# One layout of PSUM banks for the whole program, and the second block's seven products each in a bank of its own

## The chip, the cores and the metric

The kernel runs on one core of a Trainium2 chip. The metric is the time of one execution in microseconds (us) on the device, as the median of several runs. The engines are named as the profile names them: PE (TensorE, matrix products; PEld is its loading of weights), DVE (VectorE), ACT (ScalarE), POOL (GpSimd) and SP (SyncE, which issues the DMAs). Products accumulate in PSUM, which has eight banks of 128 x 512 fp32 numbers here; PE writes them, DVE and ACT read them.

## The reference

Two transformer-like blocks of two layers each run one after the other on 512 tokens of width 1024, in fp32. The first block mixes differential attention with a linear recurrence and ends each layer with a gated feed-forward part. The change concerns only the second block:

```python
for l in range(DEPTH):                               # DEPTH = 2
    mix = hybrid_mixer(x, positions, ...)
    x = layer_norm(ALPHA * x + mix, ...)
    cross = memory_cross_attention(x, mem, ...)
    x = layer_norm(ALPHA * x + cross, ...)
    h = jnp.square(jax.nn.relu(x @ w_ff1[l]))         # 1024 -> 4096
    x = layer_norm(ALPHA * x + h @ w_ff2[l], ...)     # 4096 -> 1024
```

## The kernel before

Activations lie transposed, as eight tiles of 128 features by 512 tokens. An fp32 product is made of three matmuls on float32r operands: high times high, high times low, low times high (`mm3`, L105 to L108). So each weight tile of 128 x 1024 is loaded by a DMA on SP, its high part cast on ACT (`whi`) and its low part subtracted on DVE (`wlo`); the normalised activations have their high and low parts too (`xh_all`, `xl_all`).

The feed-forward part of a layer works in four parts of 1024 hidden features each. A part computes its hidden features (the up products), passes them through relu and square into the pairs `y0` to `y3`, and then runs eight down products of 24 matmuls of 512 columns, which add into the residual `hall` (L750). Most up products go by Strassen's scheme in Winograd's form: two weight tiles and the activations are cut into quarters, and seven products of quarters take the place of eight. `halves4` (L146) makes the sums of weights, on POOL (L155 to L158), and their high and low parts. `turn_operand` (L1180) makes the sums of activations once per layer: for k from 0 to 3, POOL forms `tt` (L1189 to L1192), ACT casts its high part `th` and DVE its low part `tl` (L201, L202). `tt` has one buffer, so the second k waits until the first is cast. `seven` (L172) runs the products: each is 12 matmuls of 256 columns, 84 in all. Parts 1 to 3 have four sevens each. Part 0 begins with four plain products (`up`, L1209), three of them in halves of 256 tokens, since the norm before it finishes its halves one after the other, and has two sevens: fourteen per layer, twenty-eight in all.

A framework schedules the instructions of each engine into one order ahead of time, gives tiles their buffers in rotation and adds the semaphores. Each engine runs its own list strictly in order. PSUM banks come from a pool by name: three banks `mm`, two `sc`, and one each of `tr`, `av` and `bc`. The feed-forward part of the second block has a pool of its own, `psum_f`: three pairs of banks `two`, one `av` and one `bc`. It is opened at L1226, and the usual layout is opened again after layer 0 (L1234). A new pool hands out nothing until the last reader of the old one's banks is done. Within `psum_f`, `bank("mm")` hands out a pair in two halves, one per product, and a pair is free when both halves have been read. Part 0 leaves an odd count of halves in use, so from there on one pair is held over from the last down product of a part to the first of the next, and two pairs are left for the sevens.

In `seven`, the first product goes to `av`, and ACT copies it into `u`. The other six fill three pairs, which DVE reads two banks at a time: L190 (products 1 and 2, named p26), L193 (p57, and L194 of 256 columns) and L197 (p34). With two pairs, p34 takes the pair that p26 of the same seven had.

Of the kernel before, what the change touches and what calls it, by code (L numbers as in the profile page):

```python
# [46 lines left out]
def both_blocks(ctx: ExitStack, tc: tile.TileContext, xT, cst, par1, w1in, w1out, w1gu, w1dn, wgate,  # L47
# [2 lines left out]
    consts = ctx.enter_context(tc.tile_pool(name="consts", bufs=1))  # L50
    wpool = ctx.enter_context(tc.tile_pool(name="w", bufs=1))
    res = ctx.enter_context(tc.tile_pool(name="res", bufs=1))
    banks = ExitStack()
    psum = None

    def open_psum(name):
        nonlocal psum, banks, paired, halves
        paired, halves = name == "psum_f", None
        banks.close()
        banks = ExitStack()  # L60
        psum = banks.enter_context(tc.tile_pool(name=name, bufs=1, space=bass.MemoryType.PSUM))

    open_psum("psum")
    EARLY = 4
    BANKS = {"mm": 3, "sc": 2, "tr": 1, "av": 1, "bc": 1}
    EXTRA = {"mix1": None, "ff1": None, "mix2": "tr", "cross": "tr", "ff2": None}
    extra, turns, paired = None, {}, False

    ALL = [(0, 264), (264, 528)]
    REAL = [(16, 528)]  # L70
# [36 lines left out]
        nc.tensor.matmul(ps, wh, xl, start=False, stop=False)  # L107
        nc.tensor.matmul(ps, wl, xh, start=False, stop=last)  # L108

    halves = None  # L110

    def bank(name):
        nonlocal halves
        if name == "mm" and paired:
            if halves is None:
                got = psum.tile([128, 2, 512], F32, name="two", bufs=3)
                halves = got[:, 1]
                return got[:, 0]
            got, halves = halves, None
            return got  # L120
        n = turns[name] = turns.get(name, 0) + 1
        if name == extra and n % (BANKS[name] + 1) == 0:
            name = "bc"
        return psum.tile([128, 512], F32, name=name, bufs=BANKS[name])
# [12 lines left out]
            got.append((ps[:, :b - a], a, b))  # L137
        return got

    def twice(p):  # L140
        return p[:, None, :].to_broadcast([128, 2, p.shape[1]])

    def pair_of_banks():
        return psum.tile([128, 2, 512], F32, name="two", bufs=3)

    def halves4(pool, w1, w2):  # L146


        r1 = wpool.tile([128, 8, 128], F32, name="wraw", bufs=3)
        nc.sync.dma_start(r1, w1)  # L150
        r2 = pool.tile([128, 8, 128], F32, name="wraw2", bufs=2)
        nc.sync.dma_start(r2, w2)
        s = pool.tile([128, 8, 128], F32, name="ws", bufs=1)
        s4 = pool.tile([128, 4, 128], F32, name="ws4", bufs=1)
        nc.gpsimd.tensor_add(s[:, 4:], r2[:, :4], r2[:, 4:])  # L155
        nc.gpsimd.tensor_sub(s[:, :4], s[:, 4:], r1[:, :4])
        nc.gpsimd.tensor_sub(r2[:, :4], r1[:, :4], r2[:, :4])
        nc.gpsimd.tensor_sub(s4, r1[:, 4:], s[:, :4])  # L158
        got = []
        for x in (r1, s, r2, s4):  # L160
            if x is s4:
                hi = pool.tile([128, 4, 128], F32R, name="wh4", bufs=1)
                lo = pool.tile([128, 4, 128], F32R, name="wl4", bufs=1)
            else:
                hi = wpool.tile([128, 8, 128], F32R, name="whi", bufs=3)
                lo = wpool.tile([128, 8, 128], F32R, name="wlo", bufs=3)
            nc.scalar.copy(hi, x)  # L167
            (nc.gpsimd if x is s4 else nc.vector).tensor_sub(lo, x, f(hi))  # L168
            got += [(hi[:, o:o + 4], lo[:, o:o + 4]) for o in range(0, hi.shape[1], 4)]
        return got  # L170

    def seven(pool, w, x, n):  # L172


        a11, a12, s2, s1, s3, a22, s4 = w
# [3 lines left out]
            for k in range(4):  # L179
                mm3(ps, w[0][:, k], w[1][:, k], x[0][k], x[1][k], k == 0, k == 3)  # L180

        e = pool.tile([128, 4, n], F32, name="quarters", bufs=2)
        u = pool.tile([128, n], F32, name="u1", bufs=2)
        p1 = bank("av")[:, :n]
        p26, p57, p34 = (pair_of_banks()[:, :, :n] for _ in range(3))
        product(p1, a11, b11)
        nc.scalar.copy(u, p1)
        product(p26[:, 0], a12, b21)
        product(p26[:, 1], s2, t2)
        nc.vector.tensor_add(e[:, 0:4:3], p26, twice(u))  # L190
        product(p57[:, 0], s1, t1)
        product(p57[:, 1], s3, t3)
        nc.vector.tensor_add(e[:, 1:3], p57, twice(e[:, 3]))  # L193
        nc.vector.tensor_add(e[:, 3], p57[:, 0], e[:, 2])  # L194
        product(p34[:, 0], s4, b22)
        product(p34[:, 1], a22, t4)
        nc.vector.tensor_add(e[:, 1:3], p34, e[:, 1:3])  # L197
        return e

    def split(hi, lo, x):  # L200
# [493 lines left out]
    def two(t, k, a, b):  # L694
        return t[:, k:k + 2, a:b]

    def products(ms, spans, w, xs, evac):
        for sp in spans:
            for m in ms:
# [15 lines left out]
    with blk2:  # L715
# [135 lines left out]
        for l in range(2):  # L851
# [320 lines left out]

            with ExitStack() as ffn:
                share("ff2")
                open_psum("psum_f")
                ff = ffn.enter_context(tc.tile_pool(name="ff", bufs=1))
                before = ln
                ln = Norm(ff, LN_G + 16, LN_B + 16, l == 1)
# [21 lines left out]
                for part in range(4):  # L1200
# [20 lines left out]
                    for i in range(0 if part else 2, 4):  # L1221
                        with ExitStack() as order:
                            if part == 0:
                                for ins in after:
                                    order.enter_context(tc.issue_after(ins.ins))
                            w = halves4(ff, ups[part](2 * i), ups[part](2 * i + 1))  # L1226
                        e = seven(ff, w, rhs, 256)
                        squares(e.rearrange("p a b -> p (a b)"), *(t.rearrange("p a b -> p (a b)") for t in yp[i]))
                    phase(8, lambda m: w2f2[l, m, :, 8 * part:8 * part + 8], ys,
                          lambda m, p, a, b: ln.add(m, p, a, b, part == 0, part == 3),  # L1230
                          tail=3 if part == 3 else 0,
                          close=lambda *x: ln.close(*x, ahead=[] if l else [(wins[1], m) for m in HEAD]))
            if l == 0:
                open_psum("psum_m")  # L1234
            else:
                banks.close()


def _tiles(w):
# [106 lines left out]
```

## Time and profile before

| | |
|---|---|
| median of 3 runs | 2922.9 us (2922.8 to 2923.22) |
| profiled execution | 2924.1 us, span 2922.3 us, clock 0.981 |
| PE busy | 2775.8 us, 95% of the span |
| PEld busy | 2464.4 us, 84% |
| DVE busy | 1875.1 us, 64% |
| ACT busy | 1308.7 us, 45% |
| POOL busy | 520.8 us, 18% |
| chain that ended last | PE 79%, DVE 10%, issue 4%, ACT 4%, POOL 2% |

PE is busy nearly all the time, so what an edit is worth is read from the places where PE waits. In a row of the timeline, the bracket at the end gives how long the engine stood idle before the instruction, and which instruction ended the wait. Busy times of PE are from modelled ends, so the distance between the starts of matmuls says more than their durations.

### The profile page before, as it was taken

What the parts mean: (1) busy time and instruction counts of PE and PEld (TensorE: products, weight loads), DVE (VectorE), ACT (ScalarE), POOL (GpSimd) and SP (SyncE); (2) the same over time, 40 slices, a digit from 0 to 9 for tenths busy, and PEclk for the clock granted to TensorE, in tenths of its full rate; (3) what the DMA queues carried; (4) which work ended last, traced back from release to release, by engine and by line L of the source; (5) the groups of instructions that cost most, each with busy time, mean ns of one, the idle gap of its engine ahead of it and who ended that gap; (6) DMA issues with size and microseconds to landing.
All of it is one profiled execution on the core that took longest, in us unless ns stands there. A gap on an engine that the chain in (4) does not pass through costs nothing.

```text
span 2922.3 us, 45493 instructions
## 1 busy us (share of the span) xinstructions
PE 2775.8 (95%) x17556; PEld 2464.4 (84%) x17556; DVE 1875.1 (64%) x3662; ACT 1308.7 (45%) x2246; POOL 520.8 (18%) x521
## 2 busy tenths in 40 slices
PE   8989999999999999999999969999899999799998
PEld 7989999999877888887889868888777897688887
DVE  7887434457887444469976564556789775655555
ACT  6665222236665222236755343344456553434433
POOL 0111000000120000012120152233322200533442
PEclk9999999999999999999999989999899999899999
DMA  4232322333323333336233213332253241132322
GB/s 149 82 82 82 93 89 87 94 99 90 95 73 106 94 93 98 92 108 173 80 96 124 66 64 96 94 104 85 66 159 107 76 148 57 63 94 94 101 80 66
DMA packets 96505, 277.35 MB, mean 95 GB/s; under 512 B 13345, under 2 KB 20001, under 8 KB 96289
## 3 DMA queue, kind: packets, MB, share of 16 engines
q1 hardware_dynamic: 96288, 274.45, 31.1%
q8 instruction: 139, 2.28, 0.3%
q14 instruction: 78, 0.63, 0.1%
HBM read 241.82 MB, written 2.10 MB: 83 GB/s over the span
## 4 chain that ended last, share of the span: by engine, by line
PE 79%; DVE 10%; issue 4%; ACT 4%; POOL 2%; DMA 1%; SPq 0%; ACTq 0%; DVEq 0%; POOLq 0%
PE mm L107 17%; PE mm L108 17%; PE mm L106 17%; PE two L106 6%; PE two L107 6%; PE two L108 6%; PE av L106 1%; PE av L107 1%; PE av L108 1%; DVE wlo L102 1%; PE av L241 1%; ACT whi L167 1%; DVE isc L973 1%; DVE hall L804 1%; POOL quarters L1213 1%
## 5 line engine op out<-in xcount | busy, mean ns | idle before, releaser
L100 ACT CAST whi<-wraw 128x1024 fp32r<-128x1024 f32 (+2 forms) x404 | 406.7, 1007 | 836.1 <-PE mm L107 485.6
L106 PE MATMUL mm<-xh_all,whi 128*128 128x264 f32 (+2 forms) x2192 | 719.7, 329 | 13.5 <-ACT xh_all L340 6.7
L107 PE MATMUL mm<-xl_all,whi 128*128 128x264 f32 (+2 forms) x2192 | 720.1, 329 | 0.5 <-DVE xl_all L341 0.5
L108 PE MATMUL mm<-xh_all,wlo 128*128 128x264 f32 (+2 forms) x2192 | 717.9, 328 | 0.0
L102 DVE TENSOR_TENSOR wlo<-wraw,whi 128x1024 fp32r<-128x1024 f32 (+2 forms) x381 | 472.2, 1240 | 114.2 <-ACT whi L100 112.0
L106 PEld LDWEIGHTS mm<-xh_all,whi 128*128 128x128 f32 x2192 | 415.6, 190 | 46.0 <-ACT xh_all L340 6.7
L108 PEld LDWEIGHTS mm<-xh_all,wlo 128*128 128x128 f32 x2192 | 416.5, 190 | 30.0
L107 PEld LDWEIGHTS mm<-xl_all,whi 128*128 128x128 f32 x2192 | 415.4, 190 | 31.3 <-DVE xl_all L341 1.0
L107 PE MATMUL mm<-yl,whi 128*128 128x264 f32 (+1 forms) x528 | 169.3, 321 | 0.1
L108 PE MATMUL mm<-yh,wlo 128*128 128x264 f32 (+1 forms) x528 | 169.3, 321 | 0.0
L106 PE MATMUL mm<-yh,whi 128*128 128x264 f32 (+1 forms) x528 | 168.3, 320 | 0.0
L106 PE MATMUL two<-xh_all,whi 128*128 128x256 f32 (+1 forms) x336 | 101.3, 301 | 26.0 <-ACT quarters L1212 18.4
L673 DVE TENSOR_TENSOR su<-mm,rbc 128x264 f32<-128x264 f32 (+1 forms) x66 | 34.2, 519 | 139.8 <-PE mm L108 139.8
L682 DVE TENSOR_TENSOR hall<-hall,mm 128x264 f32<-128x264 f32 (+1 forms) x72 | 37.0, 514 | 119.9 <-PE mm L108 119.9
L750 DVE TENSOR_TENSOR hall<-hall,two 128x512 f32<-128x512 f32 (+1 forms) x54 | 33.8, 627 | 121.5 <-PE two L108 121.2
L107 PEld LDWEIGHTS mm<-yl,whi 128*128 128x128 f32 x528 | 99.2, 188 | 8.8 <-DVE yl L202 0.6
L108 PEld LDWEIGHTS mm<-yh,wlo 128*128 128x128 f32 x528 | 99.2, 188 | 7.3
L106 PEld LDWEIGHTS mm<-yh,whi 128*128 128x128 f32 x528 | 98.9, 188 | 7.6
L168 DVE TENSOR_TENSOR wlo<-wraw,whi 128x1024 fp32r<-128x1024 f32 x56 | 84.1, 1502 | 29.3 <-ACT whi L167 27.3
L108 PE MATMUL two<-xh_all,wlo 128*128 128x256 f32 (+1 forms) x336 | 100.1, 298 | 2.4 <-DVE wlo L168 2.4
L668 DVE TENSOR_TENSOR sg<-mm,rbc 128x264 f32<-128x264 f32 (+1 forms) x66 | 34.0, 517 | 103.2 <-PE mm L108 101.6
L107 PE MATMUL two<-xl_all,whi 128*128 128x256 f32 (+1 forms) x336 | 100.1, 298 | 0.0
(692 smaller groups left out, 7093.7 us busy)
## 6 DMA issues: line engine op xcount, KB each, us to landing
wraw<-w2f SPq DMA_DIRECT2D x128, 512.0 KB, 3.9
wraw<-w1gu SPq DMA_DIRECT2D x88, 512.0 KB, 3.5
wraw<-w2in SPq DMA_DIRECT2D x44, 512.0 KB, 3.8
wraw<-w1in SPq DMA_DIRECT2D x40, 512.0 KB, 3.5
wraw<-w2mkv SPq DMA_DIRECT2D x32, 512.0 KB, 3.8
wraw<-w1dn SPq DMA_DIRECT2D x32, 448.0 KB, 3.3
wraw<-w1out SPq DMA_DIRECT2D x32, 256.0 KB, 2.8
wraw<-w1dn SPq DMA_DIRECT2D x16, 512.0 KB, 3.5
```

The lines of the kernel that those rows point to most:

```text
L100: nc.scalar.copy(hi[:, :kt], raw[:, :kt])
L102: (eng or nc.vector).tensor_sub(lo[:, :kt], raw[:, :kt], f(hi[:, :kt]))
L106: nc.tensor.matmul(ps, wh, xh, start=first, stop=False)
L107: nc.tensor.matmul(ps, wh, xl, start=False, stop=False)
L108: nc.tensor.matmul(ps, wl, xh, start=False, stop=last)
L167: nc.scalar.copy(hi, x)
L168: (nc.gpsimd if x is s4 else nc.vector).tensor_sub(lo, x, f(hi))
L241: nc.tensor.matmul(ps[:ch, 2 * j:2 * j + 2], x[:, a + ch * j:a + ch * j + ch], rhs[:, :2], start=e == 0, stop=e == len(xs) - 1)
L668: nc.vector.tensor_mul(sg[:, a:b], p, r2[:, a:b])
L673: nc.vector.tensor_mul(su[:, a:b], p, r2[:, a:b])
L682: nc.vector.tensor_add(h[m][:, a:b], h[m][:, a:b], p)
L750: nc.vector.tensor_add(X(m, a, b), X(m, a, b), p)
```

## The change

`open_psum` is gone, with the pairs and the halves. One pool of the usual layout serves the whole program. In `seven` each of the seven products has a bank of its own, in the order `tr`, `mm`, `sc`, `mm`, `sc`, `mm`, `sc`, and DVE reads them by seven additions of 256 columns in place of four (three of 512 columns and one of 256). ACT still copies the first. `twice` only moves; `by_pool=True` at the one call of `halves4` leaves its work where it was. The lines of the core:

```diff
-    open_psum("psum")
+    psum = ctx.enter_context(tc.tile_pool(name="psum", bufs=1, space=bass.MemoryType.PSUM))
...
     def bank(name):
-        nonlocal halves
-        if name == "mm" and paired:
-            if halves is None:
-                got = psum.tile([128, 2, 512], F32, name="two", bufs=3)
-                halves = got[:, 1]
-                return got[:, 0]
-            got, halves = halves, None
-            return got
...
-        p1 = bank("av")[:, :n]
-        p26, p57, p34 = (pair_of_banks()[:, :, :n] for _ in range(3))
+        p1, p2, p6, p5, p7, p3, p4 = (bank(t)[:, :n] for t in ("tr", "mm", "sc", "mm", "sc", "mm", "sc"))
         product(p1, a11, b11)
         nc.scalar.copy(u, p1)
-        product(p26[:, 0], a12, b21)
-        product(p26[:, 1], s2, t2)
-        nc.vector.tensor_add(e[:, 0:4:3], p26, twice(u))
-        product(p57[:, 0], s1, t1)
-        product(p57[:, 1], s3, t3)
-        nc.vector.tensor_add(e[:, 1:3], p57, twice(e[:, 3]))
-        nc.vector.tensor_add(e[:, 3], p57[:, 0], e[:, 2])
-        product(p34[:, 0], s4, b22)
-        product(p34[:, 1], a22, t4)
-        nc.vector.tensor_add(e[:, 1:3], p34, e[:, 1:3])
+        product(p2, a12, b21)
+        nc.vector.tensor_add(e[:, 0], p2, u)
+        product(p6, s2, t2)
+        nc.vector.tensor_add(e[:, 3], p6, u)
+        product(p5, s1, t1)
+        nc.vector.tensor_add(e[:, 1], p5, e[:, 3])
+        product(p7, s3, t3)
+        nc.vector.tensor_add(e[:, 2], p7, e[:, 3])
+        nc.vector.tensor_add(e[:, 3], p5, e[:, 2])
+        product(p3, s4, b22)
+        nc.vector.tensor_add(e[:, 1], p3, e[:, 1])
+        product(p4, a22, t4)
+        nc.vector.tensor_add(e[:, 2], p4, e[:, 2])
...
-                open_psum("psum_f")
...
-            if l == 0:
-                open_psum("psum_m")
-            else:
-                banks.close()
```

In the changed file the lines stand some 20 to 30 earlier: `mm3` is L96 to L98, the split L177 and L178, the seven readings L162, L164, L166, L168, L169, L171 and L173. The change also gives the scheduler another order, since products that had to wait for a new pool need not. The names in the rows below are the program's tiles with their numbers.

PE at the entry of the feed-forward part of layer 0. `bc` receives the two broadcasts of the norm's second half of tokens (from `nmu`, the means, and `nwy`, the reciprocal roots); `two` are the first up products. Before:

```order
L789 MATMUL av_17641<-one2_74,accq_17180 128x2
L789 MATMUL av_17641<-one2_74,nsq_17607 128x2
L799 MATMUL bc_17642<-cs_68,nmu_17651 128x128 x2
L799 MATMUL bc_17642<-cs_68,nwy_17659 128x128 x2
L106 MATMUL two_17724<-xh_all_70,whi_17541 128x256
L107 MATMUL two_17724<-xl_all_71,whi_17541 128x256
L108 MATMUL two_17724<-xh_all_70,wlo_17543 128x256
```

After, around the second of the two broadcasts (`mm_17780` is the third up product on the first half of tokens, `mm_17810` and `mm_17840` are products on the second half):

```order
L98 MATMUL mm_17780<-xh_all_70,wlo_17613 128x256
L96 MATMUL mm_17780<-xh_all_70,whi_17611 128x256
L97 MATMUL mm_17780<-xl_all_71,whi_17611 128x256
L98 MATMUL mm_17780<-xh_all_70,wlo_17613 128x256
L96 MATMUL mm_17780<-xh_all_70,whi_17611 128x256
L778 MATMUL bc_17642<-cs_68,nwy_17659 128x128 x2
L97 MATMUL mm_17780<-xl_all_71,whi_17611 128x256
L98 MATMUL mm_17780<-xh_all_70,wlo_17613 128x256
L96 MATMUL mm_17810<-xh_all_70,whi_17541 128x256
L96 MATMUL mm_17840<-xh_all_70,whi_17577 128x256
```

The 72 matmuls of the first three up products on the first half of tokens have moved ahead into the norm; 44 of them stand between the two broadcasts, where nothing stood.

DVE at the same place, in the chain of small operations that ends in `nwy` (`hall` is the residual, `quarters` the up product after relu and square). Before:

```order
L217 TENSOR_TENSOR nwt_17660<-nwy_17659 128x4
L219 TENSOR_TENSOR nwt_17660<-nwt_17660,nwv_17652 128x4
L221 TENSOR_SCALAR nwt_17660<-nwt_17660 128x4
L223 SCALAR_TENSOR_TENSOR nwu_17661<-nwt_17660 128x4
L226 SCALAR_TENSOR_TENSOR nwu_17661<-nwu_17661,nwt_17660 128x4 x2
L228 SCALAR_TENSOR_TENSOR nwy_17659<-nwu_17661,nwy_17659 128x4
L820 SCALAR_TENSOR_TENSOR hall_67<-hall_67,par2_12982,bc_17642 128x256 x2
```

After:

```order
L193 TENSOR_TENSOR nwt_17660<-nwy_17659 128x4
L178 TENSOR_TENSOR y0l_17713<-quarters_17745,y0h_17712 128x256
L195 TENSOR_TENSOR nwt_17660<-nwt_17660,nwv_17652 128x4
L197 TENSOR_SCALAR nwt_17660<-nwt_17660 128x4
L199 SCALAR_TENSOR_TENSOR nwu_17661<-nwt_17660 128x4
L202 SCALAR_TENSOR_TENSOR nwu_17661<-nwu_17661,nwt_17660 128x4 x2
L178 TENSOR_TENSOR y0l_17713<-quarters_17775,y0h_17712 128x256
L204 SCALAR_TENSOR_TENSOR nwy_17659<-nwu_17661,nwy_17659 128x4
L799 SCALAR_TENSOR_TENSOR hall_67<-hall_67,par2_12982,bc_17642 128x256 x2
```

The low parts of the first two up products (`y0l`) now stand inside the chain, so `nwy` comes after both.

DVE in the second seven of part 1 of layer 0, up to its last reading of PSUM (`wlo` are low parts of weights, `y0l` the low part of the seven before). Before:

```order
L168 TENSOR_TENSOR wlo_18637<-wraw2_18620,whi_18636 128x1024
L168 TENSOR_TENSOR wlo_18754<-wraw_18743,whi_18753 128x1024
L202 TENSOR_TENSOR y0l_18486<-quarters_18519,y0h_18485 128x1024
L190 TENSOR_TENSOR quarters_18644<-two_18647,u1_18645 128x2x256
L168 TENSOR_TENSOR wlo_18758<-ws_18747,whi_18757 128x1024
L193 TENSOR_TENSOR quarters_18644<-two_18648,quarters_18644 128x512
L194 TENSOR_TENSOR quarters_18644<-two_18648,quarters_18644 128x256
L197 TENSOR_TENSOR quarters_18644<-two_18649,quarters_18644 128x512
```

After:

```order
L142 TENSOR_TENSOR wlo_18658<-wraw2_18641,whi_18657 128x1024
L162 TENSOR_TENSOR quarters_18665<-mm_18668,u1_18666 128x256
L142 TENSOR_TENSOR wlo_18781<-wraw_18770,whi_18780 128x1024
L178 TENSOR_TENSOR y0l_18501<-quarters_18534,y0h_18500 128x1024
L164 TENSOR_TENSOR quarters_18665<-sc_18669,u1_18666 128x256
L142 TENSOR_TENSOR wlo_18785<-ws_18774,whi_18784 128x1024
L166 TENSOR_TENSOR quarters_18665<-mm_18670,quarters_18665 128x256
L168 TENSOR_TENSOR quarters_18665<-sc_18671,quarters_18665 128x256
L171 TENSOR_TENSOR quarters_18665<-mm_18672,quarters_18665 128x256
L169 TENSOR_TENSOR quarters_18665<-mm_18670,quarters_18665 128x256
L173 TENSOR_TENSOR quarters_18665<-sc_18673,quarters_18665 128x256
```

The order of the casts is the same; the one reading of two banks ahead of the `ws` cast has become L162, ahead of two casts, and L164, behind them.

## Rows read from the trace of the kernel before

**Rows 1.** Stretches: busy us and instructions per engine, TensorE clock, DMA.

```profile
1700.00:1760.00 60.00, 44.48 (x288) 42.26 (x289) 29.48 (x36) 27.27 (x50) 35.89 (x35) 0.82 0.13 39
1862.00:1905.00 43.00, 43.00 (x222) 36.33 (x221) 17.34 (x19) 10.40 (x11) 11.91 (x8) 1.00 0.31 96
1820.20:1831.60 11.40, 10.36 (x88) 10.16 (x87) 9.01 (x8) 6.80 (x9) 8.30 (x6) 1.00 0.30 93
1706.85:1728.10 21.25, 12.84 (x83) 12.43 (x82) 5.94 (x7) 6.02 (x12) 16.40 (x18) 0.74 0.00 0
```

**Rows 2.** Waits of PE: us in total, times, longest.

```profile
PE two L106 <- DVE quarters L190: 18.0, 14, 2.9
```

**Rows 3.** PE in time, part 1 of layer 0: start, duration, idle and its releaser.

```profile
1810.04 0.28 PE L106 MATMUL av<-xh_all,whi 128*128 128x256 f32 x1
...
1820.05 0.28 PE L106 MATMUL av<-xh_all,whi 128*128 128x256 f32 x1
...
1828.48 0.39 PE L106 MATMUL two<-xh_all,wh 128*128 128x256 f32 x1 [1.04 <-DVE quarters L190]
```

**Rows 4.** DVE in time, the same stretch, second seven.

```profile
1824.34 1.25 DVE L168 TENSOR_TENSOR wlo<-wraw,whi 128x1024 fp32r<-128x1024 f32 x1 [0.99 <-ACT whi L167]
1825.51 2.32 DVE L202 TENSOR_TENSOR y0l<-quarters,y0h 128x1024 fp32r<-128x1024 f32 x1
1827.75 0.68 DVE L190 TENSOR_TENSOR quarters<-two,u 128x512 f32<-128x512 f32 x1
```

**Rows 5.** By tile: quarters, ns min/median/max, first and last start.

```profile
L190 DVE TENSOR_TENSOR quarters<-two,u x28: 676/682/685, 1750.5 to 2853.1; 128x512 f32<-128x512 f32 x28
...
L194 DVE TENSOR_TENSOR quarters<-two,quarters x28: 423/424/425, 1753.0 to 2855.5; 128x256 f32<-128x256 f32 x28
L197 DVE TENSOR_TENSOR quarters<-two,quarters x28: 690/692/692, 1755.9 to 2857.0; 128x512 f32<-128x512 f32 x28
```

**Rows 6.** PE in time, entry of the feed-forward part, layer 0.

```profile
1702.50 0.55 PE L106 MATMUL two<-xh_all,whi 128*128 128x256 f32 x1 [3.83 <-DVE hall L820]
...
1722.72 0.58 PE L106 MATMUL two<-xh_all,whi 128*128 128x256 f32 x1 [8.41 <-ACT quarters L1212]
1723.10 0.41 PE L107 MATMUL two<-xl_all,whi 128*128 128x256 f32 x1
1723.31 0.41 PE L108 MATMUL two<-xh_all,wlo 128*128 128x256 f32 x1
...
1755.74 0.28 PE L106 MATMUL av<-xh_all,whi 128*128 128x256 f32 x1
```

**Rows 7.** Groups by line and shape, POOL, from 1706.8 to 1728.

```profile
L1213 POOL TENSOR_TENSOR quarters<-quarters 128x256 f32<-128x256 f32 x3 | 2.8, 940 | 2.5 <-ACT quarters L1212 2.5
...
L1189 POOL TENSOR_TENSOR tt<-hall 128x256 f32<-128x256 f32 x3 | 2.2, 732 | 0.0
...
L155 POOL TENSOR_TENSOR ws<-wraw 128x512 f32<-128x512 f32 x1 | 1.3, 1290 | 0.0
```

**Rows 8.** DVE in time, the same entry.

```profile
1693.52 0.47 DVE L822 SCALAR_TENSOR_TENSOR xl_all<-hall,par,xh_all 128x256 fp32r<-128x256 f32 x1
...
1697.76 0.16 DVE L228 SCALAR_TENSOR_TENSOR nwy<-nwu,nwy 128x4 f32<-128x4 f32 x1
...
1705.76 0.47 DVE L822 SCALAR_TENSOR_TENSOR xl_all<-hall,par,xh_all 128x256 fp32r<-128x256 f32 x1
...
1727.12 0.96 DVE L202 TENSOR_TENSOR tl<-tt,th 128x768 fp32r<-128x768 f32 x1 [2.30 <-ACT th L201]
```

**Rows 9.** ACT in time, the same entry.

```profile
1726.26 0.83 ACT L201 CAST th<-tt 128x768 fp32r<-128x768 f32 x1 [1.97 <-POOL tt L1192]
```

**Rows 10.** PE in time, exit of the feed-forward part, layer 0.

```profile
2094.57 0.55 PE L106 MATMUL mm<-xh_all,whi 128*128 128x256 f32 x1 [3.82 <-DVE hall L820]
...
2114.57 0.28 PE L108 MATMUL mm<-xh_all,wlo 128*128 128x256 f32 x1
```

**Rows 11.** DVE in time, the same exit.

```profile
2096.83 0.48 DVE L822 SCALAR_TENSOR_TENSOR xl_all<-hall,par,xh_all 128x256 fp32r<-128x256 f32 x1
```

More of the change, by code (lines that the diff above doesn't have):

```diff
@@ L52, in both_blocks @@
     res = ctx.enter_context(tc.tile_pool(name="res", bufs=1))
[L53 to L58, printed above, removed]
-        banks.close()
-        banks = ExitStack()
-        psum = banks.enter_context(tc.tile_pool(name=name, bufs=1, space=bass.MemoryType.PSUM))
-    open_psum("psum")
+    psum = ctx.enter_context(tc.tile_pool(name="psum", bufs=1, space=bass.MemoryType.PSUM))
     EARLY = 4
@@ L66, in both_blocks @@
     EXTRA = {"mix1": None, "ff1": None, "mix2": "tr", "cross": "tr", "ff2": None}
-    extra, turns, paired = None, {}, False
+    extra, turns = None, {}
     ALL = [(0, 264), (264, 528)]
@@ L108, in mm3 @@
         nc.tensor.matmul(ps, wl, xh, start=False, stop=last)
-    halves = None
     def bank(name):
-        nonlocal halves
-        if name == "mm" and paired:
-            if halves is None:
-                got = psum.tile([128, 2, 512], F32, name="two", bufs=3)
-                halves = got[:, 1]
-                return got[:, 0]
-            got, halves = halves, None
-            return got
         n = turns[name] = turns.get(name, 0) + 1
@@ L138, in proj, with halves4 @@
         return got
[L140 to L146, printed above, removed]
+    def halves4(pool, w1, w2, by_pool=False):
         r1 = wpool.tile([128, 8, 128], F32, name="wraw", bufs=3)
@@ L167, in halves4, with seven @@
             nc.scalar.copy(hi, x)
-            (nc.gpsimd if x is s4 else nc.vector).tensor_sub(lo, x, f(hi))
+            (nc.gpsimd if x is s4 and by_pool else nc.vector).tensor_sub(lo, x, f(hi))
             got += [(hi[:, o:o + 4], lo[:, o:o + 4]) for o in range(0, hi.shape[1], 4)]
         return got
-    def seven(pool, w, x, n):
+    def seven(pool, w, x, n, bufs):
         a11, a12, s2, s1, s3, a22, s4 = w
@@ L180, in product @@
                 mm3(ps, w[0][:, k], w[1][:, k], x[0][k], x[1][k], k == 0, k == 3)
-        e = pool.tile([128, 4, n], F32, name="quarters", bufs=2)
+        e = pool.tile([128, 4, n], F32, name="quarters", bufs=bufs)
         u = pool.tile([128, n], F32, name="u1", bufs=2)
-        p1 = bank("av")[:, :n]
-        p26, p57, p34 = (pair_of_banks()[:, :, :n] for _ in range(3))
+        p1, p2, p6, p5, p7, p3, p4 = (bank(t)[:, :n] for t in ("tr", "mm", "sc", "mm", "sc", "mm", "sc"))
         product(p1, a11, b11)
         nc.scalar.copy(u, p1)
-        product(p26[:, 0], a12, b21)
-        product(p26[:, 1], s2, t2)
-        nc.vector.tensor_add(e[:, 0:4:3], p26, twice(u))
-        product(p57[:, 0], s1, t1)
-        product(p57[:, 1], s3, t3)
-        nc.vector.tensor_add(e[:, 1:3], p57, twice(e[:, 3]))
-        nc.vector.tensor_add(e[:, 3], p57[:, 0], e[:, 2])
-        product(p34[:, 0], s4, b22)
-        product(p34[:, 1], a22, t4)
-        nc.vector.tensor_add(e[:, 1:3], p34, e[:, 1:3])
+        product(p2, a12, b21)
[11 more added lines that the diff above has]
+        nc.vector.tensor_add(e[:, 2], p4, e[:, 2])
         return e
@@ L695, in two, with twice @@
         return t[:, k:k + 2, a:b]
+    def twice(p):
+        return p[:, None, :].to_broadcast([128, 2, p.shape[1]])
     def products(ms, spans, w, xs, evac):
@@ L1225, in both_blocks @@
                                     order.enter_context(tc.issue_after(ins.ins))
-                            w = halves4(ff, ups[part](2 * i), ups[part](2 * i + 1))
-                        e = seven(ff, w, rhs, 256)
+                            w = halves4(ff, ups[part](2 * i), ups[part](2 * i + 1), True)
+                        e = seven(ff, w, rhs, 256, 2)
                         squares(e.rearrange("p a b -> p (a b)"), *(t.rearrange("p a b -> p (a b)") for t in yp[i]))
@@ L1232, in both_blocks @@
                           close=lambda *x: ln.close(*x, ahead=[] if l else [(wins[1], m) for m in HEAD]))
-            if l == 0:
-                open_psum("psum_m")
-            else:
-                banks.close()
 def _tiles(w):
```

## The prediction

> **What bounds the kernel now.** I read the page first: PE is busy for 95% of the span and makes up 79% of the chain that ended last. An edit can therefore gain only where PE stands idle or runs at its lower clock. The stretches [rows 1] say where that is in the feed-forward part. At its entry (1700 to 1760) PE is busy for 44.5 of 60 us and the granted clock is 0.82. In the second seven of part 1 (1820.2 to 1831.6) it is busy for 10.36 of 11.40 us at full clock, and in the down products after it (1862 to 1905) for 43.00 of 43 us.
>
> Then come the waits of PE. One that the change touches repeats: PE waits for L190, the reading of p26, 14 times and 18.0 us in all [rows 2]. Seven of the 14 lie in each layer: one of 2.9 us in part 0, and one of about 1.0 in the second and the third seven of each of parts 1 to 3. The timeline shows what one costs. The first seven of part 1 starts at 1810.04, the second at 1820.05 [rows 3]: 84 matmuls in 10.01 us, 0.119 each, without a stall. In the second seven p34's first matmul starts at 1828.48, after 1.04 us of idle; its 24 matmuls at 0.119 end at 1831.34, so this seven takes 11.29 us, 1.28 more. The cause stands on DVE [rows 4]: the 128x1024 cast of a weight's low part (1.25) and the low part of the seven before (2.32) are ahead of L190, which ends at 1828.43. Only then is the pair of p26 free for p34.
>
> At the entry two waits come from the pool and its pairs [rows 6]. The first up product starts at 1702.50, after 3.83 us of idle, released by L820, a reader of the old pool's banks. Then PE stands for 8.41 us until 1722.72, because the second half of a pair waits for the first half's relu (L1212), which sits on ACT behind the cast of `th`. Behind such a gap matmuls of 256 columns start 0.21 us apart (1723.10, 1723.31) in place of 0.119: the 1.2 GHz level of the clock. The second seven of part 0 starts at 1755.74. At the exit of layer 0 there is one more wait for the pool, 3.82 us, and the products that wait end at 2114.57 [rows 10].
>
> **The change, part by part.**
>
> *The sevens of parts 1 to 3.* With a bank for each product, p34's wait for p26 goes. What comes last next? By the order, the two products `p6` and `p4` share an `sc` bank, so p4 waits for L164, the reading of p6 in the same seven. L164 stands on DVE where L190 stood, behind the same two casts. Counting from the start of the second seven, L190 began at 1827.75 − 1820.05 = 7.70 [rows 3, 4]. L164 begins there too and ends 0.42 later [rows 5], at 8.12. p4 is the seventh product: its first matmul is due after six times 12 times 0.119, at 8.57. So 0.45 us is left, and no stall. The third seven starts with DVE a little later, since five readings of 0.42 now queue behind the cast of `ws`, where two came before; that takes 0.1 to 0.2 us of the margin. I count the twelve stalls as gone: 12 × 1.28 = 15.4 us. The bounds: all of it, or none, if L164 comes 1.3 us late.
>
> *DVE's own cost.* Four readings took 0.68 + 0.68 (L193 has the same shape as L190) + 0.42 + 0.69 = 2.47 us, seven of 256 columns take 7 × 0.424 = 2.97 [rows 5]: 0.49 more per seven, 13.7 us over 28. DVE was busy for 9.01 us in the second seven [rows 1]; with 9.50 it still fits into 10.01. What hides the cost is PE's products, and the cover is thin.
>
> The Trainium skill has a rule against this edit, in "VectorE: DVE Perf Modes", the section on the TRN2 errata: every DVE instruction pays a fixed price beside its elements, and one should take 512 elements or more at a time. By its figures for PSUM the three added instructions would cost an estimated 0.375 us per seven, where the rows give 0.49, so the trace bears the rule out. It becomes time only if DVE sets the pace of the sevens; that is the second rival below.
>
> *The entry.* The three `mm` banks are free early, so the first halves of three up products run inside the norm, as the order shows. Two things answer. First, `nwy` now waits on DVE for the low parts of the first two products. The last `xl_all` of the first half of tokens is done at 1693.99 [rows 8]. Some 29 matmuls of the first two products come after it, 3.5 us at 0.119 or 6.2 at 0.213; relu, square, cast and low part of one half product add 0.94 for POOL [rows 7] and three passes of about 0.4, as DVE's 256 columns take [rows 5], 2.1 in all. That is 1699.6 to 1702.3 where `nwy` stood at 1697.76 [rows 8]: the second half of the norm comes 1.8 to 4.5 us later, I take 3.2. The matmuls of the first half no longer have to follow it, and the second halves with the 512-column product need only some 13 us after the last `xl_all` (1706.23 before). So they are done at about 1722, and PE then waits for the last `tl`.
>
> Second, therefore, the sums of the activations become the bound: the first seven's p6 needs the last `th` and `tl`. Before, POOL began its part of them at 1706.85 and the last `tl` ended at 1728.08, 21.25 us later, with POOL busy for 16.40 of it [rows 1, 8]. In the new order POOL has, from the same point: four sums for the first seven and the low part of its s4 (five of 1.29), two squares ahead of the last `tt` (0.94 each), nine steps of `tt` (0.73 to 0.79), two of `t3` (0.73) and four sums for the second seven (1.29) [rows 7]. The square of 0.6 to 0.9 that stands among the first sums included, that is 11.6 + 2.7 + 6.8 + 1.5 = 22.6 us if POOL never waits. The handovers to ACT (0.83) [rows 9] and DVE (0.96) [rows 8] that POOL must wait for, and the last one, add 1.8 to 5; I take 26. The bounds are 21.25, as now, and 30.5, if the four sums beside DVE's work stretch by 1 us each, as DVE's low part of 2.32 beside L190's neighbours does. So the last `tl` ends at 1706.85 + 3.2 + 26 = 1736.1. Behind it stand five products, 60 matmuls: 25 at 0.213, since PE has been idle, and 35 at 0.119, 9.5 us. The second seven starts at 1745.6, not 1755.74 [rows 6]: 10.1 us less, and between 4 (4.5 and 30.5) and 16 (1.8 and 21.25). Layer 1 has the same entry (the same two long waits), so 20 us, 8 to 32.
>
> *The exit of layer 0.* Here too the first halves of three products go into the norm, and rope's operations into DVE's chain. The second halves now wait for the third product's first half: 43 matmuls after the first half's `xl_all`, which delays `nwy` and so the last `xl_all` (2097.31, [rows 11]) by some 2 to 5 us, to 2099 to 2102. Behind it remain about 28 matmuls, 3.3 us at 0.119 or 6 at 0.213, and the products end between 2102.6 and 2108.3, in place of 2114.6 to 2114.9 [rows 10]. I take 6 of these 6 to 12, since the weights of what follows share DVE; the lower bound is 3.
>
> *Down products.* PE does not idle there now [rows 1]: 0. Their readings (0.69) leave a bank of three free in time.
>
> The sum: 15.4 + 20 + 6 = 41.4 us. The profiled execution takes 2924.1 us, so 2882.7 by its own time; the median of the runs is 1.2 lower, so **2881.5**.
>
> **The rivals.**
>
> *The entry gives little.* POOL's chain stretches to its upper bound in both layers and the norm's delay too: 8 in place of 20, exit 3. 2922.9 − 15.4 − 11 = 2896.5. For it: the order interleaves the second seven's sums ahead of the last `tt`. Against it: 30.5 us needs POOL slowed in every 512-column sum, while the present entry shows 1.29 for L155.
>
> *The stall only moves.* DVE sets the pace in the second and third sevens: L164 comes about 1.3 us late, and the twelve stalls stay. 2922.9 − 26 = 2897. For it: 9.50 of 10.01 us busy, and DVE now waits twice for casts in each seven ([rows 4] has 0.99 for one). By the skill's page DVE would be at 9.39, which is within the seven as well. Against: the margin of 0.45 worked out above.
>
> *Slower.* p4 waits for L164 in all 28 sevens, and not only in twelve. If one more operation like the 2.32 us low part [rows 4] comes to stand ahead of L164, it ends at 10.44, 1.87 after p4 is due: 28 × 1.87 = 52.4 us lost, against 41.4 gained: about 2934. It decides from 41.4 / 28 = 1.48 us of lateness per seven, so from a DVE backlog of 1.9 us more than the rows give. Against it: no order row adds such an operation, and the 28 readings of each shape now lie within 10 ns of each other [rows 5], so other work does not stretch them.
>
> *The change does not do what it says.* The norm's new waits eat the early start and the stalls turn out to be bounded by PE's weight loads: 2922.9. Nothing in the rows speaks for it.
>
> *More.* The sums of activations keep their 21.25 us and the exit gives 10: 2922.9 − 15.4 − 32 − 10 = 2865.5.
>
> **How the numbers follow.** Chances: forecast 0.63 (its own range 2870 to 2892), entry gives little 0.14, stall moves 0.10, more 0.04, no change 0.04, slower 0.05. A measurement of this kernel cannot tell less than about 0.2% (6 us) from no change. So faster 0.91, same 0.04, slower 0.05. The range is 2864 to 2904: from the larger gain to a little above the two middle rivals.
>
> **What would show it.** Right: no wait of PE for a reading in the second and third sevens, and seven starts 10.0 us apart; the longest wait at the entry on `tl` or `th`, the second seven of part 0 some 26 + 9.5 us after POOL's `spot`; no wait for L799's `hall` in front of a first product. Wrong: waits of `sc` products for L164 or L173 in many sevens, a second half of the norm more than 5 us later than now, or POOL's sums at 2 us and more.

## The result, and the profile after

| | before | after |
|---|---|---|
| median | 2923.06 us (2922.80 to 2927.09, 4 runs) | 2880.99 us (2878.40 to 2881.76, 4 runs) |
| profiled execution, span | 2924.1 us, 2922.3 us | 2880.77 us, 2879.0 us |
| ratio to before | | 0.9851, 95% interval 0.9834 to 0.9868 |
| PE busy, DVE busy | 2775.8 us, 1875.1 us | 2765.0 us, 1900.7 us |

The change makes the kernel 1.5% faster. The forecast was 2881.5 us. That the sum is so close is partly luck: its terms were off on both sides, by up to 6 us, as the table shows. It sets the same event of both traces side by side: the start of a seven, or the first 512-column product after the exit. Up to the entry of layer 0 the trace after lies 0.4 us behind.

| stretch | forecast | measured |
|---|---|---|
| entry of layer 0, to the second seven of part 0 (1755.74, now 1747.79) | 10.1 | 8.4 |
| from there to part 3 (1983.77, now 1970.79) | 5.1 | 5.0 |
| part 3, exit, to the first 512-column product (2114.69, now 2086.82) | 8.6 | 14.9 |
| given back up to the entry of layer 1 | 0 | -1.1 |
| entry of layer 1 (2585.72, now 2550.33) | 10.1 | 8.6 |
| from there to the end | 7.7 | 7.9 |
| sum | 41.6 (41.4 with the entries rounded to 10 each) | 43.3 and 0.4 of the late start |

(The forecast's 15.4 us for twelve sevens is 2.56 per part, put where the parts lie.)

Three of PE's waits, as total, times and longest (the one for `nwy` counts the norms of the whole second block); they answer to [rows 2]:

```profile
PE sc L96 <- ACT th L177: 18.8, 4, 8.9
PE bc L778 <- DVE nwy L204: 11.1, 10, 3.7
...
PE sc L96 <- DVE quarters L164: 3.5, 6, 0.7
```

The wait for L190 is gone. In its place PE waits for L164, but only in six sevens and for 3.5 us. The entry's long wait is now one for `th`.

The sevens of part 1 on PE, in time: their starts, and the seventh product of the third one (answers to [rows 3]).

```profile
1801.57 0.28 PE L96 MATMUL tr<-xh_all,whi 128*128 128x256 f32 x1
...
1811.58 0.28 PE L96 MATMUL tr<-xh_all,whi 128*128 128x256 f32 x1
...
1821.56 0.28 PE L96 MATMUL tr<-xh_all,whi 128*128 128x256 f32 x1
...
1829.98 0.28 PE L98 MATMUL mm<-xh_all,wl 128*128 128x256 f32 x1
1830.83 0.39 PE L96 MATMUL sc<-th,whi 128*128 128x256 f32 x1 [0.57 <-DVE quarters L164]
...
1832.37 0.28 PE L96 MATMUL tr<-xh_all,whi 128*128 128x256 f32 x1
```

The first two sevens take 10.01 and 9.98 us, as forecast. The third takes 10.81: p4 was due at 1830.10 and starts at 1830.83. DVE in the same two sevens, the second (1815.86 to 1819.26) and the third (answers to [rows 4]):

```profile
1815.86 1.24 DVE L142 TENSOR_TENSOR wlo<-wraw,whi 128x1024 fp32r<-128x1024 f32 x1 [0.67 <-ACT whi L141]
1817.02 2.32 DVE L178 TENSOR_TENSOR y0l<-quarters,y0h 128x1024 fp32r<-128x1024 f32 x1
1819.26 0.41 DVE L164 TENSOR_TENSOR quarters<-sc,u 128x256 f32<-128x256 f32 x1
...
1825.95 2.26 DVE L142 TENSOR_TENSOR wlo<-wraw,whi 128x1024 fp32r<-128x1024 f32 x1 [0.89 <-ACT whi L141]
1828.13 2.32 DVE L178 TENSOR_TENSOR y1l<-quarters,y1h 128x1024 fp32r<-128x1024 f32 x1
1830.37 0.41 DVE L164 TENSOR_TENSOR quarters<-sc,u 128x256 f32<-128x256 f32 x1
```

And POOL beside the second, up to 1818.26, and the third:

```profile
1813.74 2.27 POOL L142 TENSOR_TENSOR wl<-ws,wh 128x512 fp32r<-128x512 f32 x1
1816.09 2.17 POOL L132 TENSOR_TENSOR ws<-wraw,ws 128x512 f32<-128x512 f32 x1
...
1825.81 1.31 POOL L142 TENSOR_TENSOR wl<-ws,wh 128x512 fp32r<-128x512 f32 x1
1827.20 2.16 POOL L132 TENSOR_TENSOR ws<-wraw,ws 128x512 f32<-128x512 f32 x1
```

In the second seven L164 starts 7.68 us after the seven's start, as L190 did. In the third it starts at 8.81, since the cast ahead of it takes 2.26 us in place of 1.24. POOL works beside both casts; what differs is how much of its operation was still to come when the cast began. In the second seven that operation ends at 1816.01, 0.15 us after the cast's start, in the third at 1827.12, 1.17 us after it. Each of the two casts ends 1.09 us after POOL's operation. The low parts of `y` that follow (2.32 us) end the same 1.08 and 1.09 us after POOL's next one. The readings themselves are never stretched (28 of each, minimum, median and maximum in ns; answers to [rows 5]):

```profile
L162 DVE TENSOR_TENSOR quarters<-mm,u x28: 408/412/425, 1740.5 to 2807.4; 128x256 f32<-128x256 f32 x28
...
L173 DVE TENSOR_TENSOR quarters<-sc,quarters x28: 424/425/426, 1748.0 to 2814.5; 128x256 f32<-128x256 f32 x28
```

The entry of layer 0 on PE (answers to [rows 6]):

```profile
1699.80 0.43 PE L778 MATMUL bc<-cs,nwy 128*128 128x128 f32 x2 [0.43 <-DVE nwy L204]
...
1701.35 0.62 PE L96 MATMUL mm<-xh_all,whi 128*128 128x256 f32 x3 [0.88 <-ACT xh_all L800]
...
1738.19 0.58 PE L96 MATMUL sc<-th,whi 128*128 128x256 f32 x1 [8.93 <-ACT th L177]
1739.18 0.58 PE L97 MATMUL sc<-tl,whi 128*128 128x256 f32 x1 [0.41 <-DVE tl L178]
...
1747.79 0.28 PE L96 MATMUL tr<-xh_all,whi 128*128 128x256 f32 x1
```

The first-half products have filled the norm's idle time, and `nwy`'s broadcast comes at 1699.80, 1.8 us later than before. Then PE waits for the last `th` and `tl`. POOL's queue to there, from its `spot` to the last `tt` (answers to [rows 7]):

```profile
1709.07 0.19 POOL L1197 COPY spot<-hall 128x1 f32<-128x1 f32 x1 [1.55 <-ACT hall L804]
...
1712.43 2.27 POOL L131 TENSOR_TENSOR wraw<-wraw,wraw 128x512 f32<-128x512 f32 x1
...
1724.08 1.59 POOL L1170 TENSOR_TENSOR tt<-hall,tt 128x256 f32<-128x256 f32 x1
...
1727.55 1.99 POOL L129 TENSOR_TENSOR ws<-wraw 128x512 f32<-128x512 f32 x1
...
1736.55 0.72 POOL L1170 TENSOR_TENSOR tt<-hall,tt 128x256 f32<-128x256 f32 x1
```

and the cast that ends it on DVE (answers to [rows 8]):

```profile
1738.17 0.96 DVE L178 TENSOR_TENSOR tl<-tt,th 128x768 fp32r<-128x768 f32 x1 [2.70 <-ACT th L177]
```

From 1709.07 to 1739.13 are 30.1 us, where 26 were forecast. The sum of L131, which took 1.29 us before, takes 2.27, and the 0.73 us steps of `tt` take up to 1.70. POOL is busy for 26.5 of the 28.2 us up to the last `tt`, where the forecast counted 22.6 us of work. Sums of POOL at 2 us and more were one of the prediction's signs of being wrong, and this sign appeared.

The exit of layer 0 on PE (answers to [rows 10]) and the last `xl_all` on DVE (answers to [rows 11]):

```profile
2073.91 0.43 PE L778 MATMUL bc<-cs,nwy 128*128 128x128 f32 x2 [1.29 <-DVE nwy L204]
2076.16 0.79 PE L96 MATMUL mm<-xh_all,whi 128*128 128x256 f32 x2 [1.81 <-ACT xh_all L800]
...
2086.70 0.28 PE L98 MATMUL mm<-xh_all,wlo 128*128 128x256 f32 x1
```

```profile
2081.14 0.48 DVE L801 SCALAR_TENSOR_TENSOR xl_all<-hall,par,xh_all 128x256 fp32r<-128x256 f32 x1
```

The 3.82 us of waiting for the pool are gone, and the products end 5.1 us after the last `xl_all`.

### The profile page after: what moved, and what is told of

The parts are those of the page before. It is cut to its first block, busy times and chain, and to the rows that moved or that the text cites. A ratio compares the mean times of both kernels' runs of the same rounds, so it can differ in the third digit from the quotient of the medians.

```text
span 2879.0 us, 45629 instructions
## 1 busy us (share of the span) xinstructions
PE 2765.0 (96%) x17556; PEld 2458.3 (85%) x17556; DVE 1900.7 (66%) x3746; ACT 1308.8 (45%) x2246; POOL 519.0 (18%) x521
## 5 line engine op out<-in xcount | busy, mean ns | idle before, releaser
L96 PE MATMUL mm<-xh_all,whi 128*128 128x264 f32 (+2 forms) x2416 | 782.0, 325 | 12.2 <-ACT xh_all L316 6.9
L97 PE MATMUL mm<-xl_all,whi 128*128 128x264 f32 (+2 forms) x2416 | 785.4, 326 | 2.0 <-DVE xl_all L178 0.8
L98 PE MATMUL mm<-xh_all,wlo 128*128 128x264 f32 (+2 forms) x2416 | 782.2, 325 | 1.2 <-DVE wlo L92 1.1
L96 PEld LDWEIGHTS mm<-xh_all,whi 128*128 128x128 f32 x2416 | 456.8, 190 | 45.6 <-ACT xh_all L316 6.9
L97 PEld LDWEIGHTS mm<-xl_all,whi 128*128 128x128 f32 x2416 | 457.7, 190 | 35.6 <-DVE xl_all L801 1.6
L98 PEld LDWEIGHTS mm<-xh_all,wlo 128*128 128x128 f32 x2416 | 458.8, 190 | 32.5 <-DVE wlo L92 2.1
L98 PE MATMUL mm<-yh,wlo 128*128 128x264 f32 (+1 forms) x528 | 169.4, 321 | 0.0
L96 PE MATMUL mm<-yh,whi 128*128 128x264 f32 (+1 forms) x528 | 168.3, 320 | 0.0
L729 DVE TENSOR_TENSOR hall<-hall,mm 128x512 f32<-128x512 f32 (+1 forms) x82 | 46.6, 568 | 136.8 <-PE mm L98 136.5
L142 DVE TENSOR_TENSOR wlo<-wraw,whi 128x1024 fp32r<-128x1024 f32 x56 | 95.6, 1708 | 20.0 <-ACT whi L141 19.2
L96 PEld LDWEIGHTS mm<-yh,whi 128*128 128x128 f32 x528 | 98.9, 188 | 7.7
L98 PEld LDWEIGHTS mm<-yh,wlo 128*128 128x128 f32 x528 | 99.2, 188 | 7.3
L141 ACT CAST whi<-wraw 128x1024 fp32r<-128x1024 f32 x56 | 58.7, 1048 | 76.3 <-PE mm L97 56.0
L96 PE MATMUL sc<-th,whi 128*128 128x256 f32 x224 | 65.2, 291 | 24.5 <-ACT th L177 18.8
```

What stands on the lines that cost most here:

```text
L96: nc.tensor.matmul(ps, wh, xh, start=first, stop=False)
L142: (nc.gpsimd if x is s4 and by_pool else nc.vector).tensor_sub(lo, x, f(hi))
L729: nc.vector.tensor_add(X(m, a, b), X(m, a, b), p)
```

## The experiments

All times are medians with the ratio to the kernel before in the same series; each ratio is known to about 0.0015, some 4 us. Differences of less than that are read from the traces. The lines of some variants stand about nine lines later than in the changed kernel.

**The kernel before, three pairs for the sevens.**

```diff
+        nonlocal halves
+        halves = None
         p26, p57, p34 = (pair_of_banks()[:, :, :n] for _ in range(3))
```

> The kernel before, with one edit: at the start of each seven the half-held pair is let go, so the sevens have three pairs and p34 needs no pair of its own seven. Theory (the stalls come from the pair held over): the twelve waits for L190 of about 1.0 us vanish, 12 x 1.28 = 15.4 us, and the two of 2.9 us in part 0 with the clock behind them some 3 to 4 us each: 2923 - 15 - 7 = about 2901. Rival (DVE sets the pace of these sevens, the pair is only where it shows): the wait moves to another product and 2918 to 2923 is measured.

Measured: 2910.07 us, ratio 0.9950 (0.9936 to 0.9965). The theory holds for the cause: PE has no wait for the reading of p26 left. The gain is 14.6 us where 22 were expected, and the row that says where it went is a new one in the waits of PE:

```profile
PE two L106 <- ACT y3h L203: 8.6, 8, 1.6
```

The first down product of each part now waits for the high part of the last seven's result, in all eight parts. DVE in the last seven of part 1 of this run (L192 to L199 are its readings):

```profile
1848.91 0.68 DVE L195 TENSOR_TENSOR quarters<-two,quarters 128x512 f32<-128x512 f32 x1
1849.63 0.42 DVE L196 TENSOR_TENSOR quarters<-two,quarters 128x256 f32<-128x256 f32 x1
1850.16 0.69 DVE L199 TENSOR_TENSOR quarters<-two,quarters 128x512 f32<-128x512 f32 x1
```

p34's last matmul starts at 1848.76, but its reading stands behind those of p57 and starts 1.4 us later. So the pair that was held over did cost the stalls, and 8.6 us of the 22 that their removal was to bring go to the next wait. The changed kernel does not have this wait: there p4's last matmul starts at 1842.27 and its reading, L173, at 1842.59, since the banks before it are read one by one. Its `y3h` is ready at 1846.66 and used at 1846.76, with 0.1 us to spare.

**New pool at the entries only.**

```diff
                 share("ff2")
+                open_psum("psum_f")   # same eight banks as before it
```

> The changed kernel with a new pool of the same banks opened at the entry of each feed-forward part, and none at the exit. Theory A, from the trace after (the sums of activations on POOL are the bound of the entry, whose last wait is 8.9 us for th): the products may start 3.8 us later and still be done before the last th, and the norm is spared the casts in its chain, so the time stays within 4 us of 2881. Theory B (the prediction's story, that banks free early are what the entry gains from): most of the 8.4 us per layer comes back, about 2896.

Measured: 2891.15 us, ratio 0.9886 (0.9870 to 0.9903), 10 us slower than the change: 5 per layer. Neither theory holds whole. The rows of PE:

```profile
1702.84 0.55 PE L105 MATMUL mm<-xh_all,whi 128*128 128x256 f32 x1 [3.83 <-DVE hall L808]
...
1718.39 0.39 PE L105 MATMUL mm<-xh_all,whi 128*128 128x256 f32 x1 [2.57 <-ACT quarters L1200]
...
1752.07 0.28 PE L105 MATMUL tr<-xh_all,whi 128*128 128x256 f32 x1
```

The products start as late as before the change, and PE itself, with waits of 2.6 us for the relu, becomes the bound; the sums of activations are done in time. So of the 8.4 us of an entry, 4 to 5 come from the banks being free early, and the rest from single banks in place of pairs. This rest need not come from the 8.4 us wait for the second half of a pair. The run with three pairs keeps that wait:

```profile
1724.88 0.58 PE L106 MATMUL two<-xh_all,whi 128*128 128x256 f32 x1 [8.66 <-ACT quarters L1214]
```

It loses only the 2.91 us wait for L190 in the first seven, and from the first up product to the second seven it takes 48.4 us (1704.68 to 1753.13) where 53.2 were taken before. That is 4.8 us less, so the end of that stall alone gives as much as the rest.

**New pool at the exit only.**

```diff
+            if l == 0:
+                open_psum("psum_m")
```

> The changed kernel with a new pool of the same banks opened once, at the exit of layer 0, and none at the entries. Theory (no slower chain stands beside the products there, so all of the early start counts): the 11 to 13 us that the trace after shows between the last part of layer 0 and the next layer's products come back, about 2892. Rival (that gain comes from the sevens' and pairs' end, not from the pool): within 4 us of 2881.

Measured: 2888.54 us, ratio 0.9876 (0.9861 to 0.9891): 7.5 us slower. The wait is back where it was:

```profile
2076.70 0.56 PE L105 MATMUL mm<-xh_all,whi 128*128 128x256 f32 x1 [3.83 <-DVE hall L808]
```

It is less than the 11 to 13 us expected; the rest of what the exit gained does not hang on the pool. It lies ahead of it: in the trace after, the means of the norm's second half are broadcast at 2066.69 and not 2085.09, 18.4 us earlier, while the norm's `acc` product just before the closing products came 14.9 us earlier. Between these two events PE waited for 5.6 us before and for 0.9 us after; before, 1.18 us of it was for a half of a pair (L750, at 2074.33), and the longest, 2.15 us, for `nwy` (see the last section). How the gain divides between these waits is not shown. From the `acc` product to the first 512-column product PE takes 63.8 us before, 58.9 in this run and 50.8 in the changed kernel: 4.9 us without the pool and 8.1 with it.

**New pool at both places.**

> The changed kernel with a new pool of the same banks at each entry and at the exit of layer 0: what is left of the change are the single banks in place of pairs. If the openings at the entries (10.2 us slower alone) and at the exit (7.5 us slower alone) act apart, 2881 + 17.7 = 2899. If the entry's late start and the exit's share a cause, less than that; 2892 would be the larger of the two alone.

Measured: 2900.58 us, ratio 0.9915 (0.9899 to 0.9932), 19.6 us slower than the change. The two openings act apart and add up (10.2 and 7.5). So the change consists of two parts: about 18 to 20 us for not opening pools, and 22 to 25 for single banks in place of pairs. Of the second part the run with three pairs gives 14.6 us, and its wait of 8.6 us for `y3h`, which this run does not have, is about the rest.

**p4 in the bank `av`.**

```diff
-("tr", "mm", "sc", "mm", "sc", "mm", "sc")
+("tr", "mm", "sc", "mm", "sc", "mm", "av")
```

> The changed kernel with p4 in the bank av in place of sc, so that it no longer waits for the reading of p6 in its own seven. Theory (the six remaining stalls of the third sevens, 0.57 us of idle and 0.8 us each, are p4's wait for L164 alone): 6 x 0.8 = 4.8 us less, about 2876. Rival (DVE, slowed by POOL's operations beside it, is short of time there): the wait moves to the next seven's p6 or p7, and 2880 to 2881 is measured.

Measured: 2876.80 us, ratio 0.9835 (0.9820 to 0.9850), and every run is below every run of the change. The theory holds; the starts of the second, third and fourth sevens of part 1:

```profile
1811.82 0.28 PE L96 MATMUL tr<-xh_all,whi 128*128 128x256 f32 x1
...
1821.80 0.28 PE L96 MATMUL tr<-xh_all,whi 128*128 128x256 f32 x1
...
1831.78 0.28 PE L96 MATMUL tr<-xh_all,whi 128*128 128x256 f32 x1
```

All are 9.98 us apart. DVE's casts are as slow as in the change (2.25 and 2.31 us in the third seven); nothing waits for them any more.

**No sums of weights on POOL in parts 1 to 3.** The seven products there use the unsummed weights, so what they compute differs; the operations of DVE, ACT and PE stay.

```diff
+        else:
+            s, s4 = r2, r1[:, 4:]
```

> The changed kernel without POOL's four sums of weights in parts 1 to 3 (the sevens there use unsummed weights; DVE's, ACT's and PE's work and order stay). Theory (the remaining stall of the third sevens comes from POOL beside DVE, which stretches the 1.24 us cast to 2.26 and the low part of y to 2.32): those run in 1.2 us, the waits for L164 vanish, 6 x 0.8 = 4.8 us less, about 2876. Rival (seven readings in place of four are too much for DVE by themselves): the waits stay, 2880 to 2881.

Measured: 2876.60 us, ratio 0.9832 (0.9817 to 0.9846). The theory holds. DVE ahead of the third seven's reading of p6 (L167 here):

```profile
1825.53 1.23 DVE L145 TENSOR_TENSOR wlo<-wraw,whi 128x1024 fp32r<-128x1024 f32 x1 [0.77 <-ACT whi L144]
1826.67 1.22 DVE L181 TENSOR_TENSOR y1l<-quarters,y1h 128x1024 fp32r<-128x1024 f32 x1
1827.80 0.42 DVE L167 TENSOR_TENSOR quarters<-sc,u 128x256 f32<-128x256 f32 x1
```

The cast takes 1.23 us and the low part of y 1.22, where they took 2.26 and 2.32, and the seven starts are 9.98 us apart. The cast starts 4.27 us after the third seven's start (1821.25), and 4.39 in the change, so what made L164 late there was the length of the two operations and not their start. So the stall that was left comes from POOL beside DVE, not from seven readings being too many.

**The second seven's sums behind the last sum of activations.**

```diff
-                                for ins in after:
+                                for ins in after + [turned_last] * (i == 3):
```

(`turned_last` is the last `tt` operation on POOL.)

> The changed kernel with the second seven's sums of weights in part 0 (four POOL operations, 6.0 us in the trace after) put behind the last sum of activations on POOL. Theory (at the entry POOL's queue ahead of the last tt is the bound: 8.9 us of PE's idle ends with th): the last th comes 4 to 6 us earlier in each layer, 8 to 12 us in all, about 2871. Rival (the second seven then waits for its own sums, so the time only moves): 2879 to 2882.

Measured: 2875.00 us, ratio 0.9829 (0.9814 to 0.9844), 6 us less. The theory holds for the place, with half to three quarters of the gain: PE's four waits for `th` sum to 9.0 us in place of 18.8, and the longest is 4.0 us. A new wait of 0.5 us for `xl_all` follows.

**Both, p4 in `av` and the late sums.**

> Both edits: p4 in the bank av, and the second seven's sums behind the last sum of activations. If the two act in different places they add up: 4.2 us less (as p4 in av alone gave) and what the late sums give alone, about 2867. If both live on the same shortage of DVE time: less than the sum of the two.

Measured: 2869.44 us, ratio 0.9811 (0.9794 to 0.9827). The two add up (4.2 and 6.0, together 11.6), so they act in different places. This is the fastest kernel measured: 1.9% faster than before, and 0.4% faster than the change.

**Two buffers for `tt`.**

> The changed kernel with two buffers for tt, so that POOL need not wait until the sums before are cast. Theory (POOL's own work, 22 to 27 us, sets the last th, since POOL idles for only 1.2 us between its first sum and the last tt): little gain, 2878 to 2881. Rival (the handovers from POOL to ACT and DVE and back set it): 4 us less per layer, about 2873.

Measured: 2875.43 us, ratio 0.9829 (0.9814 to 0.9843), 5.5 us less. The theory (POOL's own work alone) falls: a part of the 30 us were handovers, or the order that the scheduler makes with one buffer. The wait for `th` is gone, and p4 of the first seven waits instead, for DVE's backlog:

```profile
1742.82 0.58 PE L96 MATMUL sc<-th,whi 128*128 128x256 f32 x1 [3.32 <-DVE quarters L164]
```

```profile
1740.14 2.29 DVE L142 TENSOR_TENSOR wlo<-wraw,whi 128x1024 fp32r<-128x1024 f32 x1
1742.35 0.41 DVE L164 TENSOR_TENSOR quarters<-sc,u 128x256 f32<-128x256 f32 x1
```

**All three.**

> The changed kernel with three edits: p4 in the bank av, the second seven's sums behind the last sum of activations, two buffers for tt. Two buffers alone gave 5.5 us and left a wait of 3.3 us of p4 for L164 in the first seven of part 0, which the bank av takes away. Theory (handovers and POOL's queue are two separate parts of the entry's wait): the 4.0 us that the two edits together still waited for th shrink to 1 or 2 in each layer, about 2864. Rival (both edits take away the same wait): 2868 to 2870, as without the second buffer.

Measured: 2871.00 us, ratio 0.9813 (0.9798 to 0.9828): no better than without the second buffer, and 1 us above the rival's range, which is within the noise. The rival holds. PE has no long wait for `th` there; its largest at the entry is 4.8 us at the first seven's first product, for the cast of its weights on ACT, and it has one of the same length with two buffers alone. So the chains of the entry replace one another.

## Why the prediction was right

- *The stalls come from the pair that is held over.* Shown: with three pairs they go, without any other change of layout.
- *p4 waits for L164 with 0.45 us to spare, and the third seven keeps 0.25 to 0.35.* Right for the second seven, where no wait appears. Wrong for the third: L164 began at 8.81 us after its start, not at 7.8, since I took the durations of the second seven's casts for the third too (1.24, 2.32), while POOL's operations had moved against them: one of them had run for only 0.14 us when the first cast began, and the cast took 2.26. The sign that the sevens start 10.0 us apart holds for the first two of a part. Six stalls of 0.8 us remain, 4.8 of the 15.4 us, and the mechanism that the second rival names is there at that size.
- *Down products: 0.* Too small by 0.4 us per part: the part takes 84.62 us (1801.57 to 1886.19) where it took 86.85, and 1.8 of these 2.2 us are the sevens'. I read from PE's busy time (43.00 of 43 us) that nothing waits; the busy time has modelled ends. The waits of PE's weight loading in the same stretch of the kernel before show three small ones, for readings of pair halves:

```profile
PEld two L106 <- DVE hall L750: 0.9, 3, 0.3
```

  So a part gains 2.23 us where 2.56 were forecast. The rest of part 0, behind the start of its second seven, gains 0.5 us (53.8 in place of 54.3) that the prediction did not have, and by this the sums in the table come out nearly alike.
- *The norm at the entry comes 1.8 to 4.5 us later.* It came 1.4 us later (1699.80 against 1697.98, less the 0.4 of the late start). The granted clock stayed at 1.00 there (1688 to 1702), and POOL's square of a half product took 0.61 us, not 0.94.
- *The sums of activations become the bound of the entry, 26 us from `spot`.* The mechanism was right; 30.1 was measured, just under the upper bound of 30.5. The term that was too small is POOL's own work, 26.5 us in place of 22.6; the handovers add the other 3.5, as forecast. POOL's time in this place includes its waiting beside DVE, and the trace before already had one of the first four sums at 1.90 us (L156), while the prediction read 1.29 from L155 for all. Two smaller errors took a part back: `spot` came 1.8 us later and not 3.2, and the products behind the last `tl` took 8.7 us and not 9.5. So the gain was 8.4 and 8.6 us where 10.1 was forecast.
- *The exit: 6 of a worked out 6 to 12.* The working was better than the value taken. From the norm's `acc` product to the first 512-column product 13.0 us were gained (63.8 us before, 50.8 after). Of these, 9.5 lie where the working looked, between the broadcast of the second half's means and the end of the products (29.5 us before, 20.0 after): the norm comes later by 2.7 us, in the forecast range of 2 to 5, and the products end 5.1 us after the last `xl_all` and not 17.3. The other 3.5 us lie ahead of it, in the closing products, of which the working said nothing. 1.1 us is given back in the next layer.
- *DVE's own cost, 13.7 us by the rows, is hidden.* DVE's busy time grew by 25.6 us (1875.1 to 1900.7), of which 28 times 7 x 0.416 in place of 2.48 makes 12 us; most of the rest is casts that stand longer beside POOL (the 56 of L142 went from a mean of 1502 to 1708 ns, 11.5 us). PE's waits show 3.5 us of it. So the rule of the Trainium skill ("VectorE: DVE Perf Modes", the section on the TRN2 errata) describes the price rightly, a fixed part per instruction, and it did not decide here.
- *The slower rival* needed L164 late in all sevens; it was late in six.

## What to carry to other kernels

A pool that is opened in the middle of a program is a barrier for the engine that fills it: here 18 to 20 us for three openings, though each wait shows only 3.8 us, because the work that could run early stands behind it. When banks are handed out in pairs, count them over the whole loop: an odd number of halves left one pair unusable in every seven. And before counting on a margin of a few tenths of a microsecond on one engine, look at how another engine's work moves beside it when the period gets shorter.

## What the runs showed of the hardware

At the entry of the changed kernel a tiny operation on DVE (128x4), in the chain to `nwy`, takes as long as POOL's operation beside it:

```profile
1698.14 0.60 DVE L197 TENSOR_SCALAR nwt<-nwt 128x4 f32<-128x4 f32 x1
```

```profile
1698.10 0.61 POOL L1191 TENSOR_TENSOR quarters<-quarters 128x256 f32<-128x256 f32 x1 [1.09 <-ACT quarters L1190]
```

L197 takes 0.60 us where its kind takes 0.15 to 0.17, and it ends at 1698.74, when POOL's square ends at 1698.71. The Trainium skill says so in "SBUF — State Buffer", the section "Who interferes with whom": an instruction of DVE in a mode with two ports and one of POOL exclude each other for the whole instruction.

Operations with two tensors are held too. In the trace before, among the closing products of layer 0:

```profile
2074.66 2.26 DVE L228 SCALAR_TENSOR_TENSOR nwy<-nwu,nwy 128x4 f32<-128x4 f32 x1
```

```profile
2074.57 2.33 POOL L102 TENSOR_TENSOR wlo<-wraw,whi 128x1024 fp32r<-128x1024 f32 x1
```

L228 ends at 2076.92, 0.02 us after POOL's operation on 1024 columns, and PE waits 2.15 us for it. The low parts of 1024 columns in the sevens behave alike: whether POOL's running operation had 0.15 or 1.2 us left, they end 1.08 to 1.09 us after it, and without POOL's sums they take 1.22 to 1.23 us. The readings from PSUM stayed at 0.408 to 0.426 us in all 196. By the same section a DVE instruction outside those modes meets POOL's reads only if it has two inputs in SBUF; that fits both.
